# Moving the memory's RMS scale from the split of its input to the evictions of its keys and values

## The chip, the cores and the metric

One core of one Trainium2 chip runs the whole kernel in one launch. The metric is device time in microseconds (us) of that core, the median over runs. Engines are named as the profile names them: PE (TensorE matmuls; PEld its weight loads), DVE (VectorE), ACT (ScalarE), POOL (GpSimd), SP (the queue from which all transfers are issued).

## The reference, cut to what matters

One layer of a decoder trunk with 256 tokens, 1024 channels and 256 memory tokens, all in float32:

```python
h = rmsnorm(x, norm_w)
proj = h @ w_in                       # q/k/v of three dilation groups (A), of MoBA (B), gates, m_q, merge logits
o_a = dilated_mixture(groups, slopes_a)
o_b = moba_attention(heads(b_q), heads(b_k), heads(b_v), slopes_b)
kv = rmsnorm(mem, mem_norm_w) @ w_mem_kv
m_k, m_v = jnp.split(kv, 2, axis=-1)
o_m = memory_cross_attention(heads(m_q), heads(m_k), heads(m_v))
p_a = (o_a * silu(a_gate)) @ w_branch_a
p_b = (o_b * silu(b_gate)) @ w_branch_b
p_m = (o_m * silu(m_gate)) @ w_branch_m
x = x + (g_a * p_a + g_b * p_b + g_m * p_m) @ w_out
return rmsnorm(x, final_norm_w)
```

`rmsnorm(mem, w)` is `mem * r * w` with one number r for each memory token, r = rsqrt(mean of squares + 1e-6). Since r belongs to a token and not to a channel, it can be taken in before or after the product with `w_mem_kv`.

## The kernel before, in words

**Chunks.** All matrix products are cut into 52 chunks of weights, most of them 1 MB (128 partitions x 2048 float32), listed by `_plan` (L31 to L57) and walked by one loop (L547), i being the chunk's number. Chunks 0 to 5 are B's queries, keys and values (Bq, Bk, Bv), 6 to 10 the gates (G: two for B, two for A, one for the memory branch), 11 the memory's keys (Mk), 12 its values (Mv), 13 the memory queries (Mq, which are made of the tokens and not of the memory), 14 to 31 A's queries, keys and values, and then merge logits (L), branch products (W) and the output product (O).

**Split precision.** A float32 operand is written as the sum of a high part rounded to float32r and the rest: h = round(a), l = a - h. A chunk is 48 matmuls of 128 x 128 by 256 columns: high x high, high x low, low x high for 8 slices of the contraction and two halves n (L228 `mm_feat` with the output's features on the partitions, L249 `mm_tok` with the tokens there). `load` (L79) brings a chunk's weights from DRAM, three iterations ahead; `split_cols` (L87) makes the parts two iterations ahead: ACT casts the high part (L93), DVE subtracts (L94). Weights have three buffers for the raw form and the high part and two for the low part.

**PSUM and eviction.** A chunk's output is one PSUM tile `pj` of three. A gate chunk is taken out by a tanh on ACT (L633) and a product g on DVE (L635); queries by `split_q` (L267), keys by `split_k` (L279: four copies on ACT, four subtractions on DVE, all reading the source they are given), values by one scaled copy on ACT (L630). For B, whose input x is not yet normalised when its chunks run, the scale comes in at the eviction (`evac_b`, L531, with rb_x spread over the partitions, or rx for one token a partition).

**The memory's input.** `mem_load` (L203, iteration 5) brings mem in natural order (memn, in a slot that later holds xres, the residual for the end) and transposed (memT). `mem_norm` (L209, iteration 7) takes the sums of squares on ACT (L171), the power -1/2 on POOL (L144) and puts r on a diagonal on DVE (L175). `spread` (L178, iteration 8) multiplies that by ones on PE, so that rb_m holds r along the free dimension on all partitions. `mem_split` (L212, iterations 9 and 10) multiplies memT by its channel weight and by rb_m (DVE, eight instructions), casts the high part mh (ACT, four) and subtracts (DVE, four) to ml. mh and ml take the slots of xh and xl (tag `xr`, two buffers), which later become `og` of B and of A (L339).

**Attention.** `chain` (L472) lists the steps of each pair of heads (scores with softmax, transposes, products with the values) with a due time, and `pump` (L468) issues those that are due in the loop. B's pairs are due from iteration 12 on, the memory's (`pair_steps_m`, L436) from 16 on.

**Order.** The context is opened with `schedule_with_timeline_sim=True` (L759): the order of instructions on each engine is drawn up when the program is built and is not simply the order of the code; an instruction whose inputs are expected early can stand ahead of earlier iterations' work. On the chip each engine runs its own order and waits by semaphores.

Of the kernel before, what the change touches and what calls it, by code (L numbers as in the profile page):

```python
# [7 lines left out]
F32 = mybir.dt.float32  # L8
F32R = mybir.dt.float32r
BF16 = mybir.dt.bfloat16  # L10
AF = mybir.ActivationFunctionType
ALU = mybir.AluOpType
PSUM = bass.MemoryType.PSUM

P = 128
S = 256
# [14 lines left out]
def _plan():  # L31

    out = []
    b0 = 5120
    for i, n in enumerate(ANAMES):
        for hf in range(2):
            out.append(("B" + n, hf, "in", b0 + 512 * i + (256 * hf if i else 0)))
    for hf in range(2):
        out.append(("G", ("b", hf), "in", 6656 + 256 * hf))
    for hf in range(2):  # L40
        out.append(("G", ("a", hf), "in", 4608 + 256 * hf))
    out.append(("G", ("m", 0), "in", 7424))
    out.append(("Mk", 0, "mem", 0))
    out.append(("Mv", 0, "mem", 256))
    out.append(("Mq", 0, "in", 7168))
    for hf in range(2):
        for g in range(3):
            for i, n in enumerate(ANAMES):
                out.append(("A" + n, (hf, g), "in", 1536 * g + 512 * i + 256 * hf))
    for br, off in (("b", 1), ("m", 2), ("a", 0)):  # L50
        for hf in range(2):
            for j in range(2):
                out.append(("L", (br, 2 * hf + j), "in", 7680 + 1024 * off + 256 * (2 * hf + j)))
            out.append(("W", (br, hf), br, 512 * hf))
    for j in range(4):
        out.append(("O", j, "out", 256 * j))
    return out  # L57


PLAN = _plan()  # L60


@with_exitstack
def kernel(ctx: ExitStack, tc: tile.TileContext, wts: bass.AP, xT_d: bass.AP, memT_d: bass.AP,
                      x_d: bass.AP, mem_d: bass.AP, xr_d: bass.AP, fnw_d: bass.AP, con_d: bass.AP, out: bass.AP):
    nc = tc.nc
# [46 lines left out]
    for i in range(2):  # L113
        raws[i] = wp.tile([P, 2048], F32, tag="wraw", name=f"wraw{i}")
        src0 = wts[offs[i]:offs[i + 1]].rearrange("(p c) -> p c", p=P)
        for j in range(4):
            k = 4 * i + j
            lo, hi = 40 + S * k if k else 0, 40 + S * (k + 1)
            nc.sync.dma_start(xp[:, lo:hi], xT_d[:, lo:hi])
            n = 512 if k else S  # L120
# [20 lines left out]
    def rstd_of(ssq, name):  # L141
        ms, r = ssq[:, 2:4], ssq[:, 4:6]
        nc.vector.tensor_scalar(ms, ssq[:, 0:2], 1.0 / D, EPS, op0=ALU.mult, op1=ALU.add)  # L143
        nc.gpsimd.tensor_tensor(r, ms, half, op=ALU.pow)  # L144
        return r
# [6 lines left out]
    for k in range(KD):  # L152
        nc.scalar.activation(xh[:, k, :], xT[:, k, :], AF.Copy, scale=nw[:, k:k + 1])
        nc.vector.scalar_tensor_tensor(xl[:, k, :], xT[:, k, :], nw[:, k:k + 1], xh[:, k, :].bitcast(F32),
                                       op0=ALU.mult, op1=ALU.subtract)
# [7 lines left out]
    mnw, hb = small[:, 0:8], small[:, 8:32]  # L163
# [3 lines left out]
    def stats(nat, name):  # L167

        ssq = cp.tile([P, 6], F32, name="ssq_" + name)
        for t in range(2):  # L170
            nc.scalar.activation(nat[:, t, :], nat[:, t, :], AF.Square, accum_out=ssq[:, t:t + 1])  # L171
        r = rstd_of(ssq, name)
        dg = tp.tile([P, 2, P], F32, tag="t", name="dg_" + name)
        for t in range(2):
            nc.vector.tensor_scalar(dg[:, t, :], ident, r[:, t:t + 1], None, op0=ALU.mult)  # L175
        return r, dg
# [10 lines left out]
    rb = {}  # L187
# [13 lines left out]
    memst = {}  # L201
# [5 lines left out]
        nc.sync.dma_start(memst["T"], memT_d)  # L207

    def mem_norm():  # L209
        _, memst["dg"] = stats(memst["nat"], "m")  # L210

    def mem_split(lo, hi):  # L212
        if lo == 0:
            memst["h"] = cp.tile([P, KD, S], F32R, tag="xr", name="mh", bufs=2)
            memst["l"] = cp.tile([P, KD, S], F32R, tag="xr", name="ml", bufs=2)
        mt, mh, ml = memst["T"], memst["h"], memst["l"]
        for k in range(lo, hi):
            nc.vector.scalar_tensor_tensor(mt[:, k, :], mt[:, k, :], mnw[:, k:k + 1], rb["m"],
                                           op0=ALU.mult, op1=ALU.mult)
        for k in range(lo, hi, 2):  # L220
            nc.scalar.copy(mh[:, k:k + 2], mt[:, k:k + 2])
            nc.vector.tensor_tensor(ml[:, k:k + 2], mt[:, k:k + 2], mh[:, k:k + 2].bitcast(F32), op=ALU.subtract)


    def rtile(name):
        return rp.tile([P, 512], F32, tag="r", name=name)
# [37 lines left out]
    def halves(s):  # L264
        return slice(HD * s, HD * (s + 1)), slice(HD * (1 - s), HD * (2 - s))

    def split_q(src, scale, name):  # L267

        xs = []
        for s in range(2):  # L270
            own, other = halves(s)
            t = rp.tile([P, 512], F32R, tag="r", name=f"{name}x{s}")
            nc.scalar.mul(t[own], src[own], scale)
            nc.vector.scalar_tensor_tensor(t[other], src[own], scale, t[own].bitcast(F32), op0=ALU.mult,
                                           op1=ALU.subtract)
            xs.append(t)
        return [t.rearrange("p (f t) -> p f t", f=2) for t in xs]

    def split_k(src, name):  # L279

        ys, zs = [], []
        for s in range(2):
            own, other = halves(s)
            t = rp.tile([P, 512], F32R, tag="r", name=f"{name}y{s}")
            nc.scalar.copy(t[own], src[own])
            nc.scalar.copy(t[other], src[own])
            ys.append(t)
        for s in range(2):
            own, other = halves(s)
            z = rp.tile([P, 512], F32R, tag="r", name=f"{name}z{s}")  # L290
            nc.vector.tensor_tensor(z[own], src[own], ys[s][own].bitcast(F32), op=ALU.subtract)
            nc.vector.tensor_tensor(z[other], src[own], ys[s][own].bitcast(F32), op=ALU.subtract)
            zs.append(z)
        return [t.rearrange("p (f t) -> p f t", f=2) for t in ys + zs]
# [6 lines left out]
    qkv, gate, og, steps, ths, acc = {}, {}, {}, [], {}, {}  # L301
# [245 lines left out]
    for i, (kind, key, src, col) in enumerate(PLAN):  # L547
# [18 lines left out]
        if i in (7, 11):  # L566
            hf = (i - 7) // 4
            qkv["Bkx", hf] = split_k(qkv["Bk", hf], f"Bk{hf}")
        if i == 7:
            mem_norm()  # L570
        if i in (9, 10):
            mem_split(4 * (i - 9), 4 * (i - 8))
        nat = kind[0] == "B"
        ah, al = (XH, XL) if nat else (HH, HL)
        if src == "mem":
# [2 lines left out]
        if kind in ("W", "O"):  # L578
            pass
        else:  # L580
            if i == 0:
                pss = [pa.tile([P, 512], F32, tag=("s", "pt")[f // 2], name=f"pj0{f}") for f in range(4)]
            elif i > 1:
                ps = pj.tile([P, 512], F32, tag="pj", name=f"pj{i}")
            if i < 2:
                mm_feat_outer(pss, i, XH, XL)
                split(i + 2, 2, 4)
                split(i + 2, 3, 4)
            for n in range(2 if i > 1 else 0):
                if tok:  # L590
                    mm_tok(ps, S * n, i, [a[:, P * n:P * (n + 1)] for a in ah], [a[:, P * n:P * (n + 1)] for a in al])
                else:
                    mm_feat(ps, S * n, i, KD, S, n, ah, al)
                if n == 0:
                    pump(i, 0)
                    if i == 3:
                        rb["x"] = spread(dgx, "x")
                    if i == 8:
                        rb["m"] = spread(memst["dg"], "m")
                    if i + 2 < NCH:  # L600
                        split(i + 2, 1, 2)
# [12 lines left out]
        elif kind in ("Aq", "Ak", "Av", "Mq", "Mk", "Mv"):  # L614
            at = (kind,) + (key if kind[0] == "A" else (0,))
            if kind[1] == "q" and at[-1] == 0:
                qkv[at] = split_q(ps, -SCALE, f"{kind}{i}")
            elif kind[1] == "k" and at[-1] == 0:
                qkv[at] = split_k(ps, f"{kind}{i}")
            elif kind == "Av" and key[1] > 0:  # L620

                hf, g = key
                if g == 1:
                    stacked[hf] = tp.tile([P, 2, 2, S], F32, tag="vs", name=f"vs{hf}")
                for r in range(2):
                    nc.scalar.copy(stacked[hf][64 * (g - 1):64 * g, :, r, :],
                                   ps[64 * r:64 * (r + 1)].rearrange("p (e c) -> p e c", e=2))
            else:
                t = qkv[at] = rtile(f"{kind}{i}")
                nc.scalar.mul(t, ps, -SCALE if kind == "Aq" else 1.0)  # L630
# [5 lines left out]
        elif kind == "L":  # L636
# [3 lines left out]
            for n in range(2):  # L640
                c = off + 2 * bk + n
                nc.scalar.activation(th[:, S * n:S * (n + 1)], ps[:, S * n:S * (n + 1)], AF.Tanh, bias=hb[:, c:c + 1],
                                     scale=0.5)
        elif kind == "W":
# [6 lines left out]
            for j in range(2):  # L651
                bk = 2 * hf + j
                ps = pj.tile([P, 512], F32, tag="pj", name=f"pw{i}{j}")
# [7 lines left out]
                else:  # L661
# [4 lines left out]
                    else:  # L666
                        nc.vector.tensor_tensor(a, a, tmp, op=ALU.add)
                        mh = rp.tile([P, 2, S], F32R, tag="r", name=f"mgh{bk}")
                        ml = rp.tile([P, 2, S], F32R, tag="r", name=f"mgl{bk}")
# [19 lines left out]
                        finish(t)  # L689
        if kind == "Bv" and key == 1:  # L690
            chain([pair_steps_b(p) for p in range(4)], 2 * i + 14, 2)
        elif kind == "Mq":
            chain([pair_steps_m(p) for p in range(2)], 2 * i + 6, 2)
        elif kind == "Av" and key[1] == 2:
            chain([pair_steps_a(2 * key[0] + p) for p in range(2)], 2 * i + 2, 4)
# [67 lines left out]
```

## Time and profile before

| | |
|---|---|
| median of 3 runs (lowest to highest) | 349.41 us (348.76 to 350.09) |
| the profiled execution's own time | 349.35 us |
| its span, first to last instruction | 347.6 us |
| PE busy | 338.2 us, 97% of the span |
| DVE busy | 232.7 us, 67% |
| ACT busy | 206.8 us, 60% |
| POOL busy | 27.1 us, 8% |

A timeline row gives the start in us from the span's start, the duration in us, the engine, the line of the kernel, the operation, what it writes and reads with the shape, how many instructions were merged in the row, and in brackets the engine's idle time before it with the instruction that ended it. Matmuls overlap: a matmul's duration is longer than the step from its start to the next one's, and the step is what it costs.

### The profile page before, as it was taken

What the parts mean: (1) busy time and instruction counts of PE and PEld (TensorE: products, weight loads), DVE (VectorE), ACT (ScalarE), POOL (GpSimd) and SP (SyncE); (2) the same over time, 40 slices, a digit from 0 to 9 for tenths busy, and PEclk for the clock granted to TensorE, in tenths of its full rate; (3) what the DMA queues carried; (4) which work ended last, traced back from release to release, by engine and by line L of the source; (5) the groups of instructions that cost most, each with busy time, mean ns of one, the idle gap of its engine ahead of it and who ended that gap; (6) DMA issues with size and microseconds to landing.
All of it is one profiled execution on the core that took longest, in us unless ns stands there. A gap on an engine that the chain in (4) does not pass through costs nothing.

```text
span 347.6 us, 7107 instructions
## 1 busy us (share of the span) xinstructions
PE 338.2 (97%) x2924; PEld 323.6 (93%) x2924; DVE 232.7 (67%) x405; ACT 206.8 (60%) x367; POOL 27.1 (8%) x40
## 2 busy tenths in 40 slices
PE   8989999999999999999999999999999999999992
PEld 5989999999999988999999999999999999999882
DVE  3849999996878863537785444666453747667554
ACT  6767799575858664637856364765643465546322
POOL 2402000100001000000101000010000304000022
PEclk9999999999999999999999999999999999999997
DMA  7998788650475443354443436345235457646003
GB/s 205 317 413 329 252 352 269 238 210 19 143 275 183 138 173 123 121 219 145 128 163 133 186 130 234 124 158 191 75 123 181 135 232 241 243 138 226 0 3 122
DMA packets 12946, 63.33 MB, mean 182 GB/s; under 512 B 1393, under 2 KB 2801, under 8 KB 6641
## 3 DMA queue, kind: packets, MB, share of 16 engines
q1 hardware_dynamic: 12912, 62.88, 51.0%
q8 instruction: 23, 0.38, 0.4%
q14 instruction: 11, 0.08, 0.1%
HBM read 61.82 MB, written 1.05 MB: 181 GB/s over the span
## 4 chain that ended last, share of the span: by engine, by line
PE 90%; DMA 4%; DVE 2%; SPq 2%; ACT 1%; issue 1%; POOL 0%; POOLq 0%; DVEq 0%
PE pj L234 17%; PE pj L237 17%; PE pj L235 17%; PE pj L254 5%; PE pj L256 5%; PE pj L255 5%; PE pt L322 3%; PE pw L234 3%; PE pw L235 3%; PE pw L237 3%; DMA xn<-in_x 3%; PE y L494 2%; PE y L493 2%; PE y L495 2%; DMA wraw<-in_wts 2%; PE oa L389 1%
## 5 line engine op out<-in xcount | busy, mean ns | idle before, releaser
L94 DVE TENSOR_TENSOR wl<-wraw,wh 128x1024 fp32r<-128x1024 f32 (+2 forms) x117 | 129.7, 1145 | 65.7 <-issue 49.2
L93 ACT CAST wh<-wraw 128x1024 fp32r<-128x1024 f32 (+2 forms) x117 | 108.1, 968 | 49.5 <-PE pj L235 32.2
L234 PE MATMUL pj<-hh,wh 128*128 128x256 f32 x480 | 114.9, 281 | 0.7 <-DVE ssq_m L143 0.7
L235 PE MATMUL pj<-hl,wh 128*128 128x256 f32 x480 | 114.2, 279 | 0.2 <-DVE hl L199 0.2
L234 PEld LDWEIGHTS pj<-hh,wh 128*128 128x128 f32 x480 | 90.3, 188 | 1.8 <-PE sb L299 0.8
L235 PEld LDWEIGHTS pj<-hl,wh 128*128 128x128 f32 x480 | 90.4, 188 | 0.8 <-DVE hl L199 0.4
L237 PE MATMUL pj<-hh,wl 128*128 128x256 f32 x480 | 66.3, 279 | 0.0
L237 PEld LDWEIGHTS pj<-hh,wl 128*128 128x128 f32 x480 | 60.0, 188 | 0.0
L254 PE MATMUL pj<-wh,hh 128*128 128x256 f32 x96 | 27.0, 281 | 0.0
L256 PE MATMUL pj<-wh,hl 128*128 128x256 f32 x96 | 26.8, 279 | 0.0
L255 PE MATMUL pj<-wl,hh 128*128 128x256 f32 x96 | 26.6, 277 | 0.0
L314 ACT ACTIVATE u<-u,st 128x384 f32<-128x384 f32 (+2 forms) x32 | 16.9, 529 | 13.1 <-DVE st L308 13.1
L323 ACT COPY ptsb<-pt 128x384 f32<-128x384 f32 (+1 forms) x28 | 13.1, 497 | 10.4 <-PE pt L322 10.3
L254 PEld LDWEIGHTS pj<-wh,hh 128*128 128x128 f32 x96 | 18.0, 188 | 0.5 <-issue 0.4
L256 PEld LDWEIGHTS pj<-wh,hl 128*128 128x128 f32 x96 | 18.0, 188 | 0.4 <-issue 0.4
L255 PEld LDWEIGHTS pj<-wl,hh 128*128 128x128 f32 x96 | 18.0, 188 | 0.0
L356 POOL TENSOR_SCALAR nba<-con 128x512 f32<-128x512 f32 x8 | 5.0, 624 | 143.6 <-DVE st L308 143.2
L316 DVE TENSOR_SCALAR u<-u,st 128x256 f32<-128x256 f32 (+2 forms) x40 | 15.1, 398 | 0.6
L494 PE MATMUL y<-wl,mgh 128*128 128x512 f32 (+1 forms) x40 | 13.9, 348 | 0.0
L493 PE MATMUL y<-wh,mgh 128*128 128x512 f32 (+1 forms) x40 | 13.9, 347 | 0.0
L495 PE MATMUL y<-wh,mgl 128*128 128x512 f32 (+1 forms) x40 | 13.9, 346 | 0.0
L322 PE MATMUL pt<-con,u 128*128 128x128 f32 x88 | 13.0, 274 | 0.0
(195 smaller groups left out, 552.8 us busy)
## 6 DMA issues: line engine op xcount, KB each, us to landing
wraw<-in_wts SPq DMA_DIRECT2D x48, 1024.0 KB, 4.8
wraw<-in_wts SPq DMA_DIRECT2D x15, 256.0 KB, 5.7
xn<-in_x SPq DMA_DIRECT2D x1, 1024.0 KB, 9.0
memT<-in_memT SPq DMA_DIRECT2D x1, 1024.0 KB, 5.2
memn<-in_mem SPq DMA_DIRECT2D x1, 1024.0 KB, 8.0
xres<-in_xr SPq DMA_DIRECT2D x1, 1024.0 KB, 4.7
wraw<-in_wts SPq DMA_DIRECT2D x2, 512.0 KB, 3.2
out<-ysb SPq DMA_DIRECT2D x4, 256.0 KB, 2.0
```

Of the source, the lines that this page charges most:

```text
L93: nc.scalar.copy(whs[i][:, sl], raws[i][:, sl])
L94: lower[i] = nc.vector.tensor_tensor(wls[i][:, sl], raws[i][:, sl], whs[i][:, sl].bitcast(F32), op=ALU.subtract)
L234: nc.tensor.matmul(ps[:, lo:lo + S], wh[:, k, fs], ah[k], start=(k == 0), stop=False)
L235: nc.tensor.matmul(ps[:, lo:lo + S], wh[:, k, fs], al[k], start=False, stop=False)
L237: nc.tensor.matmul(ps[:, lo:lo + S], wl[:, k, fs], ah[k], start=False, stop=(k == kn - 1))
L254: nc.tensor.matmul(ps[:, lo:lo + S], ah[k], wh[:, k, :], start=(k == 0), stop=False)
L255: nc.tensor.matmul(ps[:, lo:lo + S], ah[k], wl[:, k, :], start=False, stop=False)
L256: nc.tensor.matmul(ps[:, lo:lo + S], al[k], wh[:, k, :], start=False, stop=(k == KD - 1))
L322: nc.tensor.transpose(ps[:, P * j:P * (j + 1)], u[:, P * c:P * (c + 1)], ident)
L493: nc.tensor.matmul(y[t, n][:, 0:w], ht, wh[:, k, cs], start=(kc == 0 and k == 0), stop=False)
L494: nc.tensor.matmul(y[t, n][:, 0:w], ht, wl[:, k, cs], start=False, stop=False)
L495: nc.tensor.matmul(y[t, n][:, 0:w], lt, wh[:, k, cs], start=False, stop=(kc == 3 and k == 1))
```

## The change

The memory queries' chunk becomes chunk 11 and the memory's keys and values 12 and 13. `mem_split` no longer uses rb_m: for each of the eight slices ACT copies memT scaled by the channel weight to mh, and DVE forms memT times that weight minus mh in one instruction. It stands in iterations 10 and 11, `mem_norm` in iteration 9, `spread` in iteration 11. The keys are multiplied by rb_m when they leave PSUM, into an SBUF tile that `split_k` then reads; the values are copied out in two halves with r as the scale of each partition. The memory's pairs are chained after the values' chunk, which is iteration 13, as the queries' was.

```diff
@@ _plan
     out.append(("G", ("m", 0), "in", 7424))
+    out.append(("Mq", 0, "in", 7168))
     out.append(("Mk", 0, "mem", 0))
     out.append(("Mv", 0, "mem", 256))
-    out.append(("Mq", 0, "in", 7168))
@@ mem_norm, mem_split
-        _, memst["dg"] = stats(memst["nat"], "m")
+        memst["r"], memst["dg"] = stats(memst["nat"], "m")
...
         for k in range(lo, hi):
-            nc.vector.scalar_tensor_tensor(mt[:, k, :], mt[:, k, :], mnw[:, k:k + 1], rb["m"],
-                                           op0=ALU.mult, op1=ALU.mult)
-        for k in range(lo, hi, 2):
-            nc.scalar.copy(mh[:, k:k + 2], mt[:, k:k + 2])
-            nc.vector.tensor_tensor(ml[:, k:k + 2], mt[:, k:k + 2], mh[:, k:k + 2].bitcast(F32), op=ALU.subtract)
+            nc.scalar.activation(mh[:, k, :], mt[:, k, :], AF.Copy, scale=mnw[:, k:k + 1])
+            nc.vector.scalar_tensor_tensor(ml[:, k, :], mt[:, k, :], mnw[:, k:k + 1], mh[:, k, :].bitcast(F32),
+                                           op0=ALU.mult, op1=ALU.subtract)
@@ the loop
-        if i == 7:
+        if i == 9:
             mem_norm()
-        if i in (9, 10):
-            mem_split(4 * (i - 9), 4 * (i - 8))
+        if i in (10, 11):
+            mem_split(4 * (i - 10), 4 * (i - 9))
...
-                    if i == 8:
+                    if i == 11:
                         rb["m"] = spread(memst["dg"], "m")
...
+            elif kind == "Mk":
+                t = rtile("Mk")
+                nc.vector.tensor_tensor(t.rearrange("p (f t) -> p f t", f=2), ps.rearrange("p (f t) -> p f t", f=2),
+                                        rb["m"][:, None, :].to_broadcast([P, 2, S]), op=ALU.mult)
+                qkv[at] = split_k(t, f"{kind}{i}")
+            elif kind == "Mv":
+                t = qkv[at] = rtile(f"{kind}{i}")
+                for n in range(2):
+                    nc.scalar.activation(t[:, S * n:S * (n + 1)], ps[:, S * n:S * (n + 1)], AF.Copy,
+                                         scale=memst["r"][:, n:n + 1])
...
-        elif kind == "Mq":
+        elif kind == "Mv":
             chain([pair_steps_m(p) for p in range(2)], 2 * i + 6, 2)
```

## Rows read from the trace of the kernel before

**Rows 1.** The page: busy us (share of the span) xinstructions of each engine.

```profile
PE 338.2 (97%) x2924; PEld 323.6 (93%) x2924; DVE 232.7 (67%) x405; ACT 206.8 (60%) x367; POOL 27.1 (8%) x40
```

**Rows 2.** Stretches: length, busy (x) of PE, PEld, DVE, ACT, POOL, clock, DMA, GB/s.

```profile
42.00:59.00 17.00, 16.59 (x144) 16.24 (x143) 16.75 (x21) 16.72 (x25) 0.00 (x0) 1.00 0.78 280
68.00:78.00 10.00, 10.00 (x84) 9.34 (x83) 10.00 (x24) 7.18 (x17) 0.81 (x2) 1.00 0.52 186
```

**Rows 3.** Waits of PE: who waited for whom, us in total, times, longest.

```profile
PE pj L234 <- DVE ssq_m L143: 0.7, 1, 0.7
```

**Rows 4.** Timeline of PE, 57 to 60 us, around the start of chunk 9.

```profile
58.50 0.27 PE L299 MATMUL sb<-Bk0z,Bq0x 128*128 128x128 f32 x1
59.49 0.36 PE L234 MATMUL pj<-hh,wh 128*128 128x256 f32 x1 [0.72 <-DVE ssq_m L143]
```

**Rows 5.** Timeline of DVE, 53 to 61 us.

```profile
53.59 0.68 DVE L291 TENSOR_TENSOR Bk1z<-Bk,Bk1y 64x512 fp32r<-64x512 f32 x1
...
56.39 2.36 DVE L94 TENSOR_TENSOR wl<-wraw,wh 128x1024 fp32r<-128x1024 f32 x2
58.67 0.68 DVE L635 SCALAR_TENSOR_TENSOR g<-thg,pj 128x512 f32<-128x512 f32 x1
```

**Rows 6.** Timeline of ACT, 50 to 60 us.

```profile
50.78 0.62 ACT L285 CAST Bk1y<-Bk 64x512 fp32r<-64x512 f32 x1
...
53.23 0.59 ACT L633 ACTIVATE thg<-pj 128x512 f32<-128x512 f32 x1
53.84 1.06 ACT L171 ACTIVATE memn<-memn 128x1024 f32<-128x1024 f32 x1
```

**Rows 7.** Timeline of DVE, 68 to 78 us: the memory's split.

```profile
68.35 3.25 DVE L218 SCALAR_TENSOR_TENSOR memT<-memT,small,rb_m 128x256 f32<-128x256 f32 x8
...
76.85 1.28 DVE L222 TENSOR_TENSOR ml<-memT,mh 128x512 fp32r<-128x512 f32 x2
```

**Rows 8.** Timeline of PE, 71.5 to 78.5 us: two of five cuts.

```profile
72.44 0.33 PE L234 MATMUL pj<-mh,wh 128*128 128x256 f32 x1
72.61 0.28 PE L254 MATMUL pj<-wh,mh 128*128 128x256 f32 x1
...
76.18 0.38 PE L235 MATMUL pj<-ml,wh 128*128 128x256 f32 x1
76.40 0.28 PE L234 MATMUL pj<-mh,wh 128*128 128x256 f32 x1
```

**Rows 9.** Groups by form: busy us, mean ns, idle before with releasers.

```profile
L154 DVE SCALAR_TENSOR_TENSOR xl<-xp,xh 128x256 fp32r<-128x256 f32 x8 | 4.5, 561 | 2.7 <-ACT xh L153 2.6
...
L153 ACT ACTIVATE xh<-xp 128x256 fp32r<-128x256 f32 x8 | 4.1, 507 | 0.9 <-DMA xp<-in_xT 0.8
...
L218 DVE SCALAR_TENSOR_TENSOR memT<-memT,small,rb_m 128x256 f32<-128x256 f32 x8 | 3.2, 476 | 0.0
...
L222 DVE TENSOR_TENSOR ml<-memT,mh 128x512 fp32r<-128x512 f32 x4 | 2.8, 718 | 0.0
...
L221 ACT CAST mh<-memT 128x512 fp32r<-128x512 f32 x4 | 2.5, 619 | 2.0 <-DVE memT L218 2.0
...
L543 DVE SCALAR_TENSOR_TENSOR Bk<-pj,rb_x 128x512 f32<-128x512 f32 x2 | 1.4, 690 | 0.0
```

**Rows 10.** Timeline of SP, 35 to 60 us: two of the transfers issued.

```profile
37.49 0.33 SPq L207 DMA_DIRECT2D memT<-in_memT  x1
...
56.05 0.38 SPq L556 DMA_DIRECT2D xres<-in_xr  x1
```

**Rows 11.** Timeline of ACT, 85 to 92 us.

```profile
88.56 0.41 ACT L341 CAST ogb<-t 128x256 fp32r<-128x256 f32 x1 [0.39 <-PE pj L255]
```

**Rows 12.** The page, transfers: count, KB each, median us from issue to landing.

```profile
memT<-in_memT SPq DMA_DIRECT2D x1, 1024.0 KB, 5.2
```

**Rows 13.** Timeline of PE, 126 to 138 us: after a memory pair's value product.

```profile
127.11 0.38 PE L234 MATMUL pj<-hh,wh 128*128 128x256 f32 x1
127.33 0.28 PE L235 MATMUL pj<-hl,wh 128*128 128x256 f32 x1
```

## The prediction

> **What bounds the kernel now.** I read the page first, then the stretches, then the waits, then the order of single instructions. TensorE (PE) is busy 338.2 of 347.6 us [rows 1], so work taken from other engines is worth only what PE loses by it. The stretches show where it can lose: VectorE (DVE) is busy 16.75 of 17 us from 42 to 59 and all of 68 to 78, while ScalarE (ACT) is full in the first and has 2.8 us to spare in the second [rows 2]. In the waits PE has one loss that concerns this change: the first matmul of chunk 9, 0.7 us, put down to ssq_m, an instruction of `mem_norm` [rows 3]. By starts it is longer: the last score matmul starts at 58.50 and at the usual step of 0.12 the next would at 58.62, but it starts at 59.49: 0.87 us [rows 4]. Chunk 9 needs one of three PSUM tiles, so what it waits for is the gate product g of chunk 6. That product stands on DVE behind the second half's key split (Bk1z, traced in iteration 11) and the 2.36 us of a weight split, and runs 58.67 to 59.35 [rows 5], though its tanh ended at 53.82 [rows 6]. So DVE's order sets this stall. The same rows show that an engine's order is not the program's: ACT too runs Bk1y (iteration 11) ahead of the tanh of iteration 6.
>
> **The change, part by part.**
>
> *The scale leaves the split.* In the old split DVE ran eight multiplies back to back in 3.25 us, only after the scale rb_m was there, at 68.35 [rows 7]; the last two subtractions ended at 78.13. PE began the key chunk in pieces meanwhile: key, value and score matmuls alternate, and the first matmul of a piece takes 0.17 to its follower at 72.44 and 0.22 at 76.18 instead of 0.12 [rows 8]. There are five such cuts between 72.4 and 78.1 (72.44, 72.90, 73.43, 76.18, 77.87), costing 0.05 to 0.10 each, together 0.3 us. The new split needs neither the statistics nor rb_m, and its first reader is the key chunk, now one chunk later: 48 matmuls at 0.12 are 5.8 us more room. I take these 0.3 us as gone. Bounds: none gone (the pieces move to the value chunk) and 0.3.
>
> *Its instructions.* DVE drops eight multiplies (3.2 us busy) and four subtractions (2.8 us) and gains eight combined ones; the nearest row is the same form in the prologue, 4.5 us for eight with waits, 0.56 each; back to back, at the old multiply's step, 3.25 [rows 9]. So DVE saves 1.5 to 2.8 us. ACT drops four casts (2.5 us) and gains eight scaled copies (4.1 us, 0.51 each): 1.6 us more [rows 9]. Both lie in 60 to 78, where ACT has 2.8 us free in ten [rows 2]; without that cover ACT's 1.6 us would delay the tanh instructions and with them a PSUM tile.
>
> *The evictions.* The keys get one DVE multiply out of PSUM, 0.69 us by the same operation on Bk [rows 9], ahead of the four copies and four subtractions, which now read SBUF. That frees the keys' PSUM tile after 0.69 us instead of after all eight; the price is 0.69 us on DVE and on the way to the memory scores, which the next chunks' matmuls hide, since the scores are due three chunks later. The values get two scaled 256-wide copies for one 512-wide: at most 2 x 0.51 - 0.62 = 0.4 us of ACT, hidden too. Where the scores were at once due, either would cost itself. One more `rp` tile is held for a moment; the 21 are enough, because two heads' pairs are scored by then.
>
> *The moves.* `mem_norm` (two squares of 1.05 us on ACT, the first at 53.84 [rows 6], ssq_m and two diagonals on DVE, one pow on POOL, whose queue holds only the pairs' bias tables behind it) goes two iterations back, past the tanh of chunk 7 and the weight casts behind it; `spread` (two matmul passes, one ACT copy) three. None is needed before the keys' eviction, iteration 12. No transfer is added and the weight loads stay at the head of their iterations with equal sizes. But the load of xres uses memn's slot: SP issued it at 56.05, right after the squares [rows 10], and SP's queue holds the weight loads behind it. With the squares later xres goes later; it is due only near the end. The value chunk now ends after the query chunk's place, so the slot that ogb inherits from mh comes free a chunk later; before, ACT waited 0.39 us for it [rows 11], and up to that I leave in the range.
>
> *The stall at 59.49.* Not shown is DVE's new order. If it stays as it is, only ssq_m goes from between the two products: the product ends 59.35, PE could start about 0.1 earlier, gain 0.1. If the products stand ahead of the weight split (not needed before the chunk's low-part matmuls, sixteen steps of 0.12 later, 61.4), the whole 0.87 us go. I take 0.87: ACT loses 2.1 us ahead of the tanh of chunk 7, the order is drawn up anew, and the named releaser leaves.
>
> **Sum.** 349.35 (this execution's own time: span 347.6 and 1.75 around it; the median of the runs is 349.41) - 0.87 - 0.3 = 348.2 us. With the bounds above (stall 0.1 to 0.87, cuts 0 to 0.3, ACT's wait up to 0.4 the other way) it lies in 348.2 to 349.6. A measurement of this kernel can tell about 0.5%, 1.75 us, from no change: below 347.7 is faster, above 351.2 slower.
>
> **Rivals.**
>
> *Slower: the split runs ahead into 42 to 59.* memT was issued at 37.49 [rows 10] and took 5.2 us [rows 12], so it is there at 42.7, and without rb_m nothing holds the new split back. It could go the way of Bk1, which ran five iterations ahead into the fullest stretch. Then eight DVE instructions, 3.25 us, stand ahead of g at 58.67, and chunk 9 waits that much longer: 352.6; with only the first half (iteration 10, ahead of Bk1's 11) 1.6: 351.0. ACT takes 4.1 us of copies there and gives back 2.1 of squares. It decides when the first combined subtraction starts before 58.67. For it: the run-ahead shown, and that DVE never rests there. Against: what it displaces (Bk1z, 2.8 us) is itself early, so the sum ahead of g may stay. [...]
>
> *Faster: the later cuts go too.* The memory pairs' steps cut the chunks at 126 to 138 in the same way; a matmul there takes 0.22 to its follower after such a step [rows 13], and I count twelve cuts of about 0.1 between 126.3 and 137.8. If DVE, lighter by about a microsecond and a half and with the keys ready early, lets those steps run whole, up to 1.2 us more go: 347.0. Seven more cuts from 101 to 124 would at most give another 0.6: 346.4. For it: DVE is what these steps wait for. Against: those cuts come long after DVE has caught up.
>
> *No effect.* DVE's order stays, the cuts only move: 349.2.
>
> **How the numbers follow.** Forecast 348.2, own range 348.2 to 349.6: 0.34; no effect, 349.2: 0.10; faster rival, 347.0 (346.4 to 347.6): 0.32; slower rival, 351.0 to 352.6: 0.24, of which 0.22 past 351.2. Faster 0.32, same 0.46, slower 0.22. The range goes from 346.6 to 351.4: it leaves out what of the slower rival lies above, and the last corner of the faster one.
>
> **What would show it.** The forecast is right if PE's wait at chunk 9 is gone, if the combined subtractions start after the products of chunks 6 and 7, and if key and value chunks run unbroken. It is wrong if those subtractions stand before 58 us, if PE waits for a product, a weight split or a PSUM tile at a later chunk, or if SP holds weight loads behind xres.

## The result and the profile after

The kernel became slower: 352.53 us (median of 15 runs, 350.99 to 354.10) against 349.54 us for before in the same runs (15, 348.76 to 352.88), ratio 1.0071, 95% interval 1.0054 to 1.0087. The profiled execution took 351.24 us with a span of 349.5, so it is 1.9 us above before's profiled 349.35 and 1.3 us below after's own median. The median and the profiled execution do not lose the same, so both parts need a cause.

The page's busy line answers to [rows 1]:

```profile
PE 338.0 (97%) x2924; PEld 323.3 (93%) x2924; DVE 231.9 (66%) x402; ACT 208.6 (60%) x372; POOL 29.3 (8%) x40
```

DVE is 0.8 us lighter and ACT 1.8 us heavier. PE has the same instructions and nearly the same busy time in a span 1.9 us longer: in this trace the loss is a wait.

The stretches, to set beside [rows 2]:

```profile
42.00:59.00 17.00, 16.82 (x147) 16.52 (x145) 16.82 (x24) 16.70 (x29) 0.00 (x0) 1.00 0.71 254
68.00:78.00 10.00, 10.00 (x89) 9.95 (x88) 7.32 (x15) 4.02 (x7) 0.00 (x0) 1.00 0.71 262
```

In the second stretch DVE is no longer full: the split is gone from it. In the first DVE is as full as it was, but with other work, and the timelines of ACT (47 to 61 us) and DVE (52 to 63 us) show which:

```profile
47.84 3.31 ACT L218 ACTIVATE mh<-memT,small 128x256 fp32r<-128x256 f32 x8
...
55.54 0.60 ACT L641 ACTIVATE thg<-pj 128x512 f32<-128x512 f32 x1
...
58.49 1.04 ACT L171 ACTIVATE memn<-memn 128x1024 f32<-128x1024 f32 x1
...
59.53 0.57 ACT L641 ACTIVATE thg<-pj 128x512 f32<-128x512 f32 x1
```

```profile
52.35 3.25 DVE L219 SCALAR_TENSOR_TENSOR ml<-memT,small,mh 128x256 fp32r<-128x256 f32 x8
55.51 2.35 DVE L94 TENSOR_TENSOR wl<-wraw,wh 128x1024 fp32r<-128x1024 f32 x2
57.90 1.39 DVE L272 SCALAR_TENSOR_TENSOR Bq1x<-Bq,Bq1x 64x512 fp32r<-64x512 f32 x2
59.30 0.68 DVE L289 TENSOR_TENSOR Bk1z<-Bk,Bk1y 64x512 fp32r<-64x512 f32 x1
59.99 0.69 DVE L290 TENSOR_TENSOR Bk1z<-Bk,Bk1y 64x512 fp32r<-64x512 f32 x1
60.71 0.69 DVE L643 SCALAR_TENSOR_TENSOR g<-thg,pj 128x512 f32<-128x512 f32 x1
61.43 0.69 DVE L289 TENSOR_TENSOR Bk1z<-Bk,Bk1y 64x512 fp32r<-64x512 f32 x1
62.13 0.69 DVE L290 TENSOR_TENSOR Bk1z<-Bk,Bk1y 64x512 fp32r<-64x512 f32 x1
```

The whole memory split, written in iterations 10 and 11, runs at 52 us, between the weight splits of chunks 8 and 9. The gate product g of chunk 6 starts at 60.71, 4.6 us after its tanh ended (55.54 + 0.60); in before it started at 58.67 [rows 5]. The squares of `mem_norm`, though now written in iteration 9, still stand ahead of the tanh of chunk 7 (the second one at 58.49, the tanh at 59.53). PE's rows around chunk 9 and its longest wait follow, against [rows 4] and [rows 3]:

```profile
58.77 0.27 PE L297 MATMUL sb<-Bk0z,Bq0x 128*128 128x128 f32 x1
...
61.54 0.36 PE L232 MATMUL pj<-hh,wh 128*128 128x256 f32 x1 [2.50 <-DVE g L643]
```

```profile
PE pj L232 <- DVE g L643: 2.5, 1, 2.5
```

From the last score matmul to chunk 9's first the step is now 61.54 - 58.77 = 2.77 us; in before it was 59.49 - 58.50 = 0.99, so it grew by 1.78. The last output matmul comes 1.88 us later (343.00 against 341.12), but it only looks as if the step were nearly all of that: chunk 6 starts 0.27 later, from there to the last memory-value product it is 0.97 more (the step's 1.78, less 0.81 got back), and from there to the end 0.65 more. The releaser is now g itself, and no longer ssq_m.

Later the change does what it says. Timeline of DVE, 78 to 90 us, and of PE behind the first half of the value chunk:

```profile
78.62 2.36 DVE L94 TENSOR_TENSOR wl<-wraw,wh 128x1024 fp32r<-128x1024 f32 x2 [2.94 <-PE pj L235]
...
86.46 0.69 DVE L618 TENSOR_TENSOR Mk<-pj,rb_m 128x512 f32<-128x512 f32 x1
```

```profile
86.59 0.82 PE L320 MATMUL pt<-con,u 128*128 128x128 f32 x6
...
88.11 0.33 PE L252 MATMUL pj<-wh,mh 128*128 128x256 f32 x1
```

DVE even rests 2.94 us, and the key chunk's matmuls run from 78.42 to 83.86 without a foreign matmul among them, the value chunk's on to 86.47; there the transposes and scores of B cut the value chunk once. SP issues xres later (56.05 in before), as expected, and PE's waits show none that follows from it:

```profile
59.65 0.38 SPq L554 DMA_DIRECT2D xres<-in_xr  x1
```

### The profile page after: what moved, and what is told of

Same layout as the page of the kernel before. It is cut to its first block, busy times and chain, and to the rows that moved or that the text cites. A ratio compares the mean times of both kernels' runs of the same rounds, so it can differ in the third digit from the quotient of the medians.

```text
span 349.5 us, 7112 instructions
## 1 busy us (share of the span) xinstructions
PE 338.0 (97%) x2924; PEld 323.3 (93%) x2924; DVE 231.9 (66%) x402; ACT 208.6 (60%) x372; POOL 29.3 (8%) x40
## 4 chain that ended last, share of the span: by engine, by line
PE 87%; DMA 4%; DVE 4%; SPq 2%; ACT 1%; issue 1%; POOL 0%; POOLq 0%; DVEq 0%
PE pj L232 17%; PE pj L235 16%; PE pj L233 16%; PE pj L252 5%; PE pj L254 5%; PE pj L253 5%; PE pt L320 3%; DMA xn<-in_x 3%; PE pw L232 3%; PE pw L233 3%; PE pw L235 3%; PE y L492 2%; PE y L491 2%; PE y L493 2%; DMA xp<-in_xT 1%; PE oa L387 1%
```

## The experiments

Nine more kernels ran, and after twice more. Since chunk 6 starts up to 2 us apart in the traces (40.37 to 42.38), they are compared from the first matmul of chunk 6 on. The table has, for each: the step from the last B score matmul to chunk 9's first ("none": the scores are not there and the chunks follow each other unbroken), from chunk 6's first matmul to the last memory-value product (om), from there to the last output matmul (y), the median, and the ratio to the runs of before taken beside it, with the 95% interval.

| kernel | step | chunk 6 to om | om to y | median | ratio |
|---|---|---|---|---|---|
| before | 0.99 | 96.60 | 203.66 | 349.54 | |
| after | 2.77 | 97.56 | 204.31 | 352.53 | 1.0071 [1.0054, 1.0087] |
| a_hold | 0.99 | 95.80 | 204.31 | 349.70 | 0.9996 [0.9974, 1.0018] |
| a_hold_dve | 0.11 | 94.91 | 204.31 | 349.43 | 0.9994 [0.9968, 1.0019] |
| a_hold_both | none | 94.86 | 204.31 | 348.78 | 0.9971 [0.9953, 0.9990] |
| b_scale | 2.23 | 96.62 | 203.66 | 351.57 | 1.0037 [1.0014, 1.0059] |
| b_swap | 1.01 | 95.20 | 203.66 | 348.51 | 0.9961 [0.9942, 0.9980] |
| b_pad1 | 3.93 | 99.65 | 203.66 | 353.66 | 1.0101 [1.0069, 1.0133] |
| b_hold_bk | none | 94.30 | 203.66 | 347.61 | 0.9945 [0.9923, 0.9968] |
| b_scale_hold | none | 95.57 | 203.91 | 348.22 | 0.9949 [0.9929, 0.9968] |
| b_swap_hold_bk | none | 94.25 | 203.90 | 348.43 | 0.9965 [0.9949, 0.9982] |
| after_again | 2.78 | 99.16 | 204.32 | 353.51 | one run |
| after_third | 2.77 | 98.98 | 204.31 | 352.44 | one run |

### The split held back: a_hold and a_hold_dve

`tanhs[i]` and `prods[i]` record the tanh and the product of gate chunk i; `behind` is an edge in the instruction order, nothing else (nested `tc.issue_after`).

```diff
-            mem_split(4 * (i - 10), 4 * (i - 9))
+            with behind(tanhs[8], prods[8]):
+                mem_split(4 * (i - 10), 4 * (i - 9))
```

In a_hold_dve the edge is `behind(prods[8])` alone, so that only DVE's subtractions are held.

> The changed kernel with one edge on ACT and one on DVE: the memory's split may not stand ahead of the tanh and the gate product of chunk 8. Theory (the split that ran ahead delays the gate product of chunk 6 and with it chunk 9): the step on PE from the last score matmul to chunk 9 falls from 2.77 us to about 1.0, as before the change, and the time to 349.0 to 349.6 (ratio to before 0.997 to 1.001). Rival (the new evictions, the swap or the later statistics cost the time): the step falls but the time stays above 351, or the step stays.

> After, with the memory's subtractions held behind the product of chunk 8 on DVE, while ACT's eight copies still run ahead. Theory (DVE's 3.25 us of subtractions delay the product; ACT's 3.31 us of copies alone would be hidden): product at about 59 us, step of PE ahead of chunk 9 of 0.9 to 1.3 us, time within 0.6 of a_hold's 349.7. Rival (ACT's copies hold up the tanh and the weights' rounding as much): product at 60.5 or later, step of 2 us or more, 351 to 352.5.

a_hold: 349.70 us, 0.1 above the expected range, and the step is before's again. PE around chunk 9, and DVE's product and subtractions:

```profile
59.06 0.27 PE L304 MATMUL sb<-Bk0z,Bq0x 128*128 128x128 f32 x1
60.05 0.36 PE L232 MATMUL pj<-hh,wh 128*128 128x256 f32 x1 [0.72 <-DVE ssq_m L143]
```

```profile
59.23 0.68 DVE L651 SCALAR_TENSOR_TENSOR g<-thg,pj 128x512 f32<-128x512 f32 x1
...
64.86 3.26 DVE L219 SCALAR_TENSOR_TENSOR ml<-memT,small,mh 128x256 fp32r<-128x256 f32 x8
```

The subtractions take the same 3.26 us, behind the product. From chunk 6 to the last om this is 97.56 - 95.80 = 1.76 us less than after, the step's 1.78. The ratio goes from 1.0071 to 0.9996: holding back the split alone gives back the whole loss. (Beside before, its 0.80 us less up to om and 0.65 more from om to y nearly cancel; the last section tells of them.)

a_hold_dve: 349.43 us, the same as a_hold within the intervals, though its copies still run ahead. ACT, DVE and PE in its trace:

```profile
47.24 3.31 ACT L218 ACTIVATE mh<-memT,small 128x256 fp32r<-128x256 f32 x8
```

```profile
56.05 0.68 DVE L296 TENSOR_TENSOR Bk1z<-Bk,Bk1y 64x512 fp32r<-64x512 f32 x1
56.75 0.68 DVE L297 TENSOR_TENSOR Bk1z<-Bk,Bk1y 64x512 fp32r<-64x512 f32 x1
57.46 0.69 DVE L651 SCALAR_TENSOR_TENSOR g<-thg,pj 128x512 f32<-128x512 f32 x1
```

```profile
58.21 0.27 PE L304 MATMUL sb<-Bk0z,Bq0x 128*128 128x128 f32 x1
58.32 0.33 PE L232 MATMUL pj<-hh,wh 128*128 128x256 f32 x1
```

So DVE's 3.25 us are the cause of the step, and ACT's 3.31 are not. The step came out smaller than expected (0.11): with the copies ahead, half of Bk1z lands behind the product, and nothing is left to wait for. The profiled run took 347.98 us; the median does not show that gain, and two of the 12 runs had a mean clock of 0.992 or less. Where those runs lose is not in this trace and stays open.

### One part alone: b_scale and b_swap

b_scale is before's plan and before's iterations with only the new `mem_split`, `memst["r"]` and the two evictions. b_swap is before with only this:

```diff
+    out.append(("Mq", 0, "in", 7168))
     out.append(("Mk", 0, "mem", 0))
     out.append(("Mv", 0, "mem", 256))
-    out.append(("Mq", 0, "in", 7168))
...
-        elif kind == "Mq":
+        elif kind == "Mv":
             chain([pair_steps_m(p) for p in range(2)], 2 * i + 6, 2)
```

> The kernel before with only the scale moved from the split to the evictions: chunk order and the iterations of statistics, spread and split as before. Theory: rb_m alone had held the split back, so the step on PE ahead of chunk 9 is about 2.8 us and the time 351 to 353, as with the whole change. Rival (swap and moved statistics cost the time): step 1.0, time about 349.5.

> Before, with the memory's key and value chunks and its query chunk in each other's place and nothing else. The DVE order ahead of chunk 9 is before's, so both theories have the step ahead of chunk 9 at 1.0 us. If the swap itself loses time behind the memory's pairs (as the 0.65 us between the last om and the last y matmul of after, a_hold and a_hold_both suggest), 350.3 to 350.7 and that stretch at 204.3; if it is neutral, 349.5 to 350.1.

b_scale alone has the wait, in the expected range of time, but only about half of the loss (1.0037 against 1.0071). PE around chunk 9 in its trace:

```profile
59.70 0.27 PE L297 MATMUL sb<-Bk0z,Bq0x 128*128 128x128 f32 x1
...
61.93 0.36 PE L232 MATMUL pj<-hh,wh 128*128 128x256 f32 x1 [1.96 <-DVE g L643]
```

Its subtractions run at 52.73, as in after, although they are written in iterations 9 and 10 and not in 10 and 11. So the place in the code does not hold them; the product with rb_m did, and taking the scale out removed it. The step is 2.23 and not the expected 2.8: counted from chunk 6's first matmul, the product starts after 19.5 us, in after after 19.6, but the last score matmul comes 0.5 us later than in after. In this one trace the longer step does not show in the sum (96.62 against before's 96.60), because fewer matmuls went at the longer of the two paces told of below (269 against 382, 0.5 us) and the rest was got back in places not traced. b_swap alone is faster than before (0.9961) and below both expectations, with the step of before and 203.66 us from om to y: the swap by itself doesn't lose the 0.65 us there.

### The wait by itself: b_pad1

Before, with one more DVE instruction ahead of the product of chunk 6, an identity; the order drawn up for it also puts the 2.35 us of chunk 10's weight split ahead of the product. Nothing of the memory's work is touched.

```diff
+            for _ in range(1 if i == 6 else 0):
+                nc.vector.tensor_tensor(th, th, th, op=ALU.max)
             g = gate[key] = rp.tile([P, 512], F32, tag="g", name=f"g{i}", bufs=5)
```

> Before, with one more DVE instruction (0.7 us, an identity on the tanh) ahead of the gate product of chunk 6; in the instruction order the product then also stands behind the split of chunk 10's weights, so it ends some 3.2 us later than in before, and nothing of the memory's work is touched. Theory (a late gate product alone makes the loss of after, whatever delays it): step of PE ahead of chunk 9 of 4.0 to 4.3 us, time before plus 3.2 in a run with a clock of 0.996, so 352.5 to 353.5, and if a long wait also costs clock later, most runs show a clock of 0.993 or less as after and b_scale do, and the median is 353.5 to 354.5. Rival (the loss of after comes from the copies, the evictions or the swap): 351 or less, and clocks as in before.

353.66 us. DVE and PE in its trace; the product of chunk 6 is the first of the two merged in the second row:

```profile
58.68 0.68 DVE L635 TENSOR_TENSOR thg<-thg 128x512 f32<-128x512 f32 x1
...
61.62 1.28 DVE L637 SCALAR_TENSOR_TENSOR g<-thg,pj 128x512 f32<-128x512 f32 x2
```

```profile
58.52 0.27 PE L299 MATMUL sb<-Bk0z,Bq0x 128*128 128x128 f32 x1
...
62.45 0.55 PE L234 MATMUL pj<-hh,wh 128*128 128x256 f32 x1 [3.65 <-DVE g L637]
```

The product starts 61.62 - 58.67 = 2.95 us later than in before and the step is 2.94 us longer: a little below what was expected, and one for one. A late product alone makes after's kind of loss, with the median in the expected range. The clock column (third from the right) of the windows behind that wait shows a second loss:

```profile
63.00:64.00 1.00, 1.00 (x7) 1.00 (x6) 1.00 (x9) 0.72 (x3) 0.38 (x1) 0.50 0.72 213
64.00:65.00 1.00, 1.00 (x7) 1.00 (x6) 1.00 (x7) 1.00 (x6) 0.52 (x2) 0.50 1.04 442
65.00:66.00 1.00, 1.00 (x7) 1.00 (x7) 1.00 (x9) 0.14 (x2) 0.00 (x0) 0.58 0.80 336
66.00:67.00 1.00, 1.00 (x11) 1.00 (x11) 0.18 (x1) 0.00 (x0) 0.00 (x0) 1.00 0.09 25
```

The granted clock is 0.50 behind that wait, with 7 matmuls a microsecond in place of 11, and 1.00 again from 66 us on.

### After once more: after_again and after_third

In after's first trace the clock stood at 1.00 behind the wait, though 10 of its 15 runs had a mean clock of 0.993 or less, against 1 of the 34 runs of before beside a_hold. The median of those ten runs is 352.79 us, of the other five 351.28.

> After once more, unchanged, for one more trace. Theory (a PE wait of 2.8 us ahead of chunk 9 is long enough that in most runs the granted clock falls behind it, as it fell to 0.50 at 63 to 65 us of b_pad1's trace behind a wait of 3.9 us): if the run's mean clock is 0.993 or less, its time is 352.2 to 354.1, and the windows from 61 to 67 us show a granted clock of 0.50 for about 2 to 3 us and no other stretch of the middle does; if it is 0.996 or more, 351.0 to 352.4 and 1.00 there. Rival (the low mean clock comes from the start of the run, or from anywhere else): 1.00 in those windows whatever the mean.

> As after_again, in case that run is of the higher clock: the same two outcomes with the same numbers.

Both had the lower mean clock, 0.993 and 0.991, and times in the expected range. Windows of after, then of after_again, then of after_third:

```profile
62.00:63.00 1.00, 1.00 (x11) 1.00 (x10) 0.96 (x3) 1.00 (x2) 0.00 (x0) 1.00 0.92 348
63.00:64.00 1.00, 1.00 (x11) 1.00 (x10) 1.00 (x8) 1.00 (x2) 0.35 (x1) 1.00 1.07 397
```

```profile
62.00:63.00 1.00, 0.83 (x7) 0.86 (x8) 0.96 (x3) 1.00 (x2) 0.00 (x0) 1.00 0.92 377
63.00:64.00 1.00, 1.00 (x9) 1.00 (x9) 0.97 (x4) 1.00 (x2) 0.00 (x0) 0.77 0.98 406
64.00:65.00 1.00, 1.00 (x7) 1.00 (x7) 1.00 (x8) 1.00 (x3) 0.62 (x2) 0.50 1.04 426
65.00:66.00 1.00, 1.00 (x6) 1.00 (x6) 1.00 (x2) 1.00 (x6) 0.92 (x2) 0.50 0.32 119
66.00:67.00 1.00, 1.00 (x7) 1.00 (x6) 1.00 (x2) 0.77 (x4) 0.89 (x1) 0.53 0.00 0
67.00:68.00 1.00, 1.00 (x11) 1.00 (x11) 1.00 (x2) 0.00 (x0) 0.00 (x0) 1.00 0.00 0
```

```profile
61.00:62.00 1.00, 0.68 (x3) 0.71 (x4) 0.96 (x3) 1.00 (x2) 0.00 (x0) 0.50 1.23 340
62.00:63.00 1.00, 1.00 (x7) 1.00 (x7) 0.97 (x4) 1.00 (x2) 0.00 (x0) 0.50 0.99 152
63.00:64.00 1.00, 1.00 (x6) 1.00 (x6) 1.00 (x10) 1.00 (x2) 0.47 (x2) 0.50 0.69 283
```

The wait ahead of chunk 9 is the same 2.8 us in all three, but in two of them PE then ran some 3 us at a granted clock of 0.50: in after_third from its return, in after_again from about a microsecond later. From the start of chunk 9 to that of chunk 10 it took 5.54 us in after, 7.16 in after_again and 6.98 in after_third. From chunk 6 to the last om they took 99.16 and 98.98 us against 97.56: 1.6 and 1.4 us, about the 1.5 between the two groups of runs. As far as three traces show, that is the rest of the median. The other runs tell only their mean clock, which is a rough sign, since in the traces of before and after the last 3.9 and 2.3 us of the span, behind the last output matmul, are at 0.50 too. Beside one of before's 34 runs with a mean clock of 0.993 or less, b_scale with its step of 2.23 us had 7 of 11 there; of b_pad1 all 5 were. Of the seven kernels with a step of 1.01 us or less, five had none of their 11 or 12 runs there, b_hold_bk one and a_hold_dve two.

### What beats both kernels

> The changed kernel with both edges: the memory's split behind chunk 8's gate, the second key split behind chunk 7's. Theory: step ahead of chunk 9 at most 0.25 us and key and value chunks unbroken, so the 348.2 us that were predicted: 347.9 to 348.6 (ratio 0.995 to 0.9975). Rival (the two gains don't add, or the change costs something of its own): 349 or more.

> The kernel before with the second half's key split (Bk1y on ACT, Bk1z on DVE) held behind the tanh and the gate product of chunk 7. Theory (the 0.87 us before chunk 9 were the gate product of chunk 6 queued on DVE behind work that had run ahead): the step of 0.99 us falls to 0.25 or less and the time by 0.6 to 0.9, to 348.6 to 348.9 (ratio 0.9975 to 0.9985). Rival (chunk 9 waits for its weight split, or the loss only moves to a later chunk): the step or the time stays, 349.5.

> Kernel of before's order of chunks with the scale brought in at the evictions, the memory's split held behind the gate of chunk 8 on ACT and DVE, and the second key split of the first stage held behind the gate of chunk 7. Theory (the gate product of chunk 6 is what the split delays, and the edges free it): no step of PE ahead of chunk 9, the memory's key and value chunks without a cut, and as the chunks' order is before's, the stretch from the last om matmul to the last y matmul is 203.7 us and not 204.3. Time 346.5 to 347.6, at or below b_hold_bk's 347.6. Rival (the moved scale itself costs time, by its evictions or the ACT copies): 348.5 or more although PE shows no step ahead of chunk 9.

> Before with the swap of the chunks and the second key split of the first stage held behind chunk 7's gate; the scale stays in the split. Theory (the step ahead of chunk 9 is what the edge takes, and it is a part of its own beside what the swap gives): no step ahead of chunk 9, the stretch from the last om matmul to the last y matmul at 203.7, and 346.5 to 347.6, at or below b_hold_bk's 347.6. Rival (the swap's gain in b_swap was the pace at which its matmuls happened to run, and does not add up): 347.6 to 348.6.

All four hold the second half's key split (Bk1) behind chunk 7's gate:

```diff
-            qkv["Bkx", hf] = split_k(qkv["Bk", hf], f"Bk{hf}")
+            with (behind(tanhs[7], prods[7]) if hf else ExitStack()):
+                qkv["Bkx", hf] = split_k(qkv["Bk", hf], f"Bk{hf}")
```

b_hold_bk is before with this alone: 347.61 us, 0.9945. DVE and PE in its trace:

```profile
53.13 0.69 DVE L643 SCALAR_TENSOR_TENSOR g<-thg,pj 128x512 f32<-128x512 f32 x1
...
56.67 0.68 DVE L298 TENSOR_TENSOR Bk1z<-Bk,Bk1y 64x512 fp32r<-64x512 f32 x1
```

```profile
56.56 0.84 PE L237 MATMUL pj<-hh,wl 128*128 128x256 f32 x6
57.24 0.28 PE L234 MATMUL pj<-hh,wh 128*128 128x256 f32 x1
```

The product starts 5.5 us earlier than in before and the stall of 0.87 us, the prediction's main term, is really there to be had: by holding the right instructions, not by this change. The median fell by more than the expected 0.6 to 0.9 us. Of the 2.30 us less from chunk 6 to om, the stall can be 0.87; about 1.0 goes with the pace (152 matmuls at the longer one, 382 in before), and the rest was not traced. With the change on top (a_hold_both adds the edges of a_hold) it is 348.78, between its two expectations; with only the scale moved and the split held as well (b_scale_hold) 348.22, between its two expectations; with only the swap (b_swap_hold_bk) 348.43, where the rival put it: the swap's gain doesn't add up. None of the three has a step ahead of chunk 9, and their intervals overlap with b_hold_bk's; none of the changed parts improves on it. In b_scale_hold, 330 matmuls from chunk 6 to om went at the longer of the two paces told of below, against 152 in b_hold_bk: 0.8 of its 1.27 us there.

## Why the prediction was wrong

**The stall at chunk 9 is the step that failed.** The prediction took 0.87 us as gone, since "ACT loses 2.1 us ahead of the tanh of chunk 7, the order is drawn up anew, and the named releaser leaves". It was drawn up anew the other way, and the squares did not leave their place ahead of that tanh either. The step grew by 1.78 us, and by 1.4 to 1.6 more in the two traces whose clock fell: in place of -0.87 the term measured +1.8 to +3.4. Naming ssq_m as what leaves was no ground for a gain; in after the wait names g, some three times as long.

**The slower rival was what happened,** in its full form: the first combined subtraction at 52.35, long before its deciding point of 58.67, with memT there by 42.8 (issued at 37.7, 5.1 us). Its price of 3.25 us and its 352.6 stand beside a median of 352.53, but that the sum agrees so well is luck, by terms that it did not have. Half of Bk1z, 1.38 us, moved behind the product, so that the product is 3.25 - 1.38 = 1.87 us later by DVE's rows and the step 1.78 longer; and the clock takes 1.4 to 1.6 us in two of three traces. The rest is 0.81 us got back up to om and 0.65 lost behind it, most of both by the two paces told of below. The argument against it, that what the subtractions displace "is itself early, so the sum ahead of g may stay", was half right and too weak: it excused a forecast that its own for-argument (nothing holds the split, and DVE never rests) should have turned. The chance of 0.24 was too low for a mechanism whose every condition stood in the rows.

**The cuts of the key chunk** are gone from it, as predicted (78.42 to 83.86 whole), and the value chunk has one, where the prediction asked for none; but the 0.3 us are not seen in the sum. From chunk 6 to the last om, after is 0.97 us longer with a step 1.78 longer, so 0.81 came back; of that the traces put 0.84 on the pace of matmuls told of below (382 steps near 0.118 in before, 196 in after, 4.5 ns each), which leaves nothing for the cuts. The score and transpose matmuls that made them stand elsewhere now: in that stretch a projection matmul follows another kind at 22 places in before and at 22 in after.

**The instructions' own costs** were right. Eight combined subtractions took 3.25 us, the value at the old multiply's step; the key eviction 0.69, the two value copies 0.8. ACT's eight copies took 3.31 us, where the prologue's row had 4.1 and the four casts of before 2.5 [rows 9]. That is more work on ACT, but not in the place that decided: in a_hold_dve the copies take the same 3.31 us from 47.24 on, and its step is 0.11 us.

**The moves** cost nothing more on PE: no wait follows xres at 59.65 or the squares, and `spread` cuts a chunk as it did in before, the first projection matmul behind it taking 0.31 us to its follower in both (66.29 in before, 75.49 in after). ACT's wait of 0.39 us for ogb, which the range left room for, did not grow into a wait of PE. **The faster rival** did not come: from the first om matmul to the last it took 10.93 us in before (126.53 to 137.46) and 11.29 in after.

A short instruction was held by a full DVE: from the end of its tanh at 56.14 to its own start at 60.71, 4.6 us, g stood behind the rest of a weight split and behind Bq1x and half of Bk1z, which PE first read at 94.6 and 94.8 us in after's trace.

## What to carry to other kernels

A dependence that looks like a cost can be what keeps work in its place: before taking one away, ask when the freed instructions could start and what stands behind them on their engine. Here a program drew up the order, and the early-ready split, written in iterations 10 and 11, went to 52.35 us, ahead of a product of iteration 6; where that fills an engine whose short instructions free the next engine's buffers, add an order edge with the change (a_hold: ratio 0.9996 in place of 1.0071). And a wait on PE can cost more than its length, as the 2.8 us here did by 1.4 to 1.6 in two traces of three: look at the granted clock behind it, in more than one trace.

## What was not expected of the hardware

**The clock behind a short wait.** After 2.8 us without a new matmul PE's granted clock was 0.50 for some 3 us in two traces of three, at a cost of 1.4 to 1.6 us; after 3.93 us in b_pad1's trace as well; after 0.99 us in before, or 2.23 in b_scale's one trace, it stayed at 1.00. In after_third the clock was already low when PE came back, in after_again PE ran for a microsecond at 1.00 before it fell. From one kernel the same wait gives both outcomes, so one trace of such a kernel can miss the loss.

**Two paces of the same matmul.** Matmuls of 256 columns at a granted clock of 1.00 go at one of two steady steps, 0.113 or 0.118 us, over dozens of them. Windows of before and then of after, projection matmuls alone, in a stretch where nothing waits:

```profile
140.00:155.00 15.00, 15.00 (x135) 15.00 (x134) 0.00 (x0) 1.83 (x4) 1.00 0.45 159
```

```profile
140.00:155.00 15.00, 15.00 (x129) 15.00 (x129) 0.00 (x0) 2.35 (x4) 1.00 0.40 141
```

135 against 129 matmuls in the same 15 us. The pace is mostly kept until a chunk ends or other matmuls come between, and after that it may be the other. It is worth up to about a microsecond between these traces, as in b_hold_bk above. From om to y all kernels with the whole change take 204.31 us against 203.66, and there about 120 more matmuls at the longer pace make some 0.54 of the 0.65; the kernels with one part take 203.66 to 203.91. What chooses the pace was not tried, and differences of a few tenths in the table should not be read without it.
